# Expert results in one row per token and choice: a plain store that skips empty slots, in place of a scatter that adds into zeroed rows

## The chip, the core and the metric

The kernel runs on one core of a Trainium2 chip. The metric is device time in microseconds (us) of one launch; the time of a kernel is the median of several runs. One more run is recorded by the hardware profiler, and all rows below come from that one.

## The reference, cut to what matters

Two blocks of two layers each work on 512 tokens of width 1024. In the first block each layer has a mixer (fox attention, then mla, a latent attention) and a mixture of 16 experts, of which each token takes 2. The second block has a hyena mixer and a differential attention.

```
def hier_moe(h, w_grp, b_grp, w_rt, b_rt, w_gate, w_up, w_down):
    ...
    e_top, e_idx = lax.top_k(in_group, TOP_K_IN_GROUP)      # 2 of 16 experts for each of 512 tokens
    w = jax.nn.softmax(e_top, axis=-1) * g_top
    expert_id = g_idx * EXPERTS_PER_GROUP + e_idx
    combine = jnp.sum(jax.nn.one_hot(expert_id, N_EXPERTS, dtype=jnp.float32) * w[..., None], axis=1)
    a = jnp.einsum('td,edf->tef', t, w_gate)
    u = jnp.einsum('td,edf->tef', t, w_up)
    hidden = jax.nn.silu(a) * u * combine[..., None].astype(t.dtype)
    out = jnp.einsum('tef,efd->td', hidden, w_down)
...
    for i in range(DEPTH):
        ...                                                  # mixer: fox attention (i = 0), mla (i = 1)
        x = x + g1 * y
        h = rmsnorm(x, ffn_norm[i]) * (1.0 + sc2) + sh2
        x = x + g2 * hier_moe(h, ...)
# second block, on x and 16 meta tokens
    for i in range(DEPTH):
        y = rmsnorm_2(h, norm_pre[i])                        # then hyena (i = 0), differential attention (i = 1)
        ...
        h = h + rmsnorm_2(y, norm_post[i])
```

Only the mixture of experts, and the step that adds its result to x, are touched by the change. In all, 512 tokens with 2 choices make 1024 weighted expert results per layer, each a row of 1024 floats (4 KB).

## The kernel before

The work runs as one stream of stages on one core: fox attention (0 to about 345 us in the profile), the layer 0 mixture (routing to 410, 16 experts to 633), mla (to 905), the layer 1 mixture (routing to 965, experts to 1180, one overflow expert to 1207), hyena (to about 1890) and differential attention. TensorE multiplies in three passes with operands split in two halves (`whi` on ACT at L125, `wlo` on DVE at L128), so each 512 KB weight tile (`raw`, loaded at L133 by the SP queue) costs a cast on ACT and one on DVE.

**The mixture of experts.** `moe_head` writes the normed tokens to a DRAM table `hd`. Each expert has 128 slots, so 16 x 128 = 2048 slots hold 1024 results, and half of them are empty. The routing makes a table `tix` with the token of every slot; empty slots point to spare rows from 512 on. For each expert, POOL gathers the 128 rows (`xg`, L1206), PE transposes and multiplies (`expert_in`, `expert_out`), ACT copies the result to `yo` (one buffer, L1092), and POOL scatters the 128 rows to the DRAM table `yd` with an adding DMA (L1093). So that the adding has something to add to, `moe_fill` writes zeros to `yd` (640 rows of 4 KB) and to the spare rows of `hd` (128 rows), for each layer, during fox attention: its loop over head groups `g` calls it at g = 1 and g = 6, on the SP queue. Experts that overflow 128 slots are run behind the 16, in a block under a run-time condition (`tc.If`) and a loop. All engines pass the end of this block only when the DMAs before it have landed.

**The handover.** `moe_sum` (L1263) loads `yd` back in four tiles of 128 tokens (`y`, 512 KB each). `moe_norm` takes each: times the gate, added to x, square sum (DVE for the first tile, ACT for the others), a power on POOL, times the gain, and then eight transposes on PE (L374, `put_T`), which give the next stage's stationary operand. This step stands behind layer 0 (in `mla`) and behind layer 1 (in hyena). Hyena's filters (`hy_filter`, lines L1350 to L1412, tables `fsk` and `fk`, ending in the store `hs<-ht` by ACT's DMA queue) are computed along with the experts. The last of them is finished behind the block under the condition, at the start of the handover.

**What sets the order.** A list scheduler orders each engine's instructions at build time; each engine then runs its own in that order. DMAs of the SP queue are issued in that order too, and an instruction that must wait holds all that stand behind it on the same queue. DMAs take one of eight semaphores (DMAHW0 to 7) in turn, so a DMA can also wait for the one that used its semaphore before. Every phase (`Phase`) lays its tiles by tag into the same SBUF columns that the phase before used, and the build adds a wait where a new tile lies over an old one that is still read.

Of the kernel before, what the change touches and what calls it, by code (L numbers as in the profile page):

```python
# [20 lines left out]
S = 512  # L21
D = 1024
NT = S // 128
KD = D // 128
EPS = 1e-6
T = 528
# [4 lines left out]
FQ = 266  # L31
# [41 lines left out]
class Model:  # L73
# [264 lines left out]
    def moe_norm(self, ys, gain, hT, c0, tags, shift=None):  # L338


        nc, ph = self.nc, self.ph
        V = nc.vector

        def add(t):
            return V.tensor_add(self.x[t], self.x[t], ys[t])
        V.tensor_mul(ys[0], ys[0], self.g2)
        add(0)
        for t in range(NT):
            x, h = self.x[t], ys[t]
# [108 lines left out]
    def fox(self):  # L458
        nc, I, sm = self.nc, self.I, self.sm
        V, A = nc.vector, nc.scalar  # L460
        bufs = dict(raw=3, whi=4, wlo=4, un=24, qkv=8, P0=2, P1=2, P2=2, P3=1, PT=3, qT=3, kk=4, bias=2, sq=2, tmp=3, res=1, ada=2)
        with Phase(self, "fox", dict(mm=2, ad=1, pv=1, sc=2, tq=1, tp=1), bufs,
# [147 lines left out]
            for g in range(8):  # L610
# [93 lines left out]
    def mla(self):  # L704
        nc, I, sm = self.nc, self.I, self.sm
        V = nc.vector
        bufs = dict(raw=3, whi=4, wlo=4, h4=4, un=10, qk=16, v=2, qT=4, P0=2, P1=2, P2=2, P3=2, PT=3, sq=2, rot=2)
        with Phase(self, "mla", dict(mm=2, pv=1, sc=2, tq=2, tp=1), bufs,
# [7 lines left out]
            ys = [ph.t([128, D], F32, "qT", "y") for _ in range(NT)]  # L716
# [195 lines left out]
    def moe_consts(self):  # L912
# [9 lines left out]
        self.past = cp.tile([128, 1], F32, name="past")  # L922
        nc.vector.tensor_scalar(self.past, self.tok1[:, 0:1], float(S), None, op0=ALU.add)
# [11 lines left out]
        self.hd = [self.dr.tile([S + 128, D], F32, name=f"hd{l}") for l in range(2)]  # L935
        self.yd = [self.dr.tile([S + 128, D], F32, name=f"yd{l}") for l in range(2)]
        self.tabd = [self.dr.tile([128, 23, 2], F32, name=f"tabd{l}") for l in range(2)]

    def moe_fill(self, l):

        nc = self.nc
        zy = self.ph.t([128, 256], F32, "sq", "zy")
        nc.vector.memset(zy, 0.0)
        z = lambda n: zy[:, None, :].to_broadcast([128, n, 256])
        v = lambda a: a.rearrange("(p i) d -> p (i d)", p=128).rearrange("p (a b) -> p a b", b=256)
        nc.sync.dma_start(v(self.yd[l]), z(20))
        nc.sync.dma_start(v(self.hd[l][S:]), z(4))

    def moe_head(self, l, rows, work, bank):
# [22 lines left out]
        nc.sync.dma_start(self.hd[l][0:S].rearrange("(t p) d -> p t d", p=128), sh[:, None, :].to_broadcast([128, NT, D]))  # L972
# [103 lines left out]
    def expert_out(self, th, dn_w, idx, yd):  # L1076
# [14 lines left out]
        for c in range(2):  # L1091
            nc.scalar.copy(yo[:, c * 512:(c + 1) * 512], acc[c])  # L1092
        nc.gpsimd.indirect_dma_start(out=yd, out_offset=bass.IndirectOffsetOnAxis(ap=idx, axis=0),  # L1093
                                     in_=yo, in_offset=None, compute_op=ALU.add)

    def moe(self, l):
# [4 lines left out]
        with Phase(self, f"moe{l}", dict(dn=2, fl=2, mm=2, tp=2), bufs,  # L1101
# [61 lines left out]
            for i, (h, s_, w) in enumerate(((h1, s1, w1), (h2, s2, w2))):  # L1163
# [9 lines left out]
                V.tensor_mul(R[:, :, 0, :], R[:, :, 0, :], b(self.tok1, 23))  # L1173
# [6 lines left out]
            tf = ph.t([128, 23, 2], F32, "tf")  # L1180
            emp = ph.t([128, 23], F32, "emp")
            V.tensor_scalar(emp, ptv[:, 0, :], 0.0, self.past, op0=ALU.is_equal, op1=ALU.mult)
            V.scalar_tensor_tensor(tf[:, :, 0], emp, -1.0, ptv[:, 0, :], op0=ALU.add, op1=ALU.add)
            tix = ph.t([128, 23], I32, "tix")
            V.tensor_copy(tix, tf[:, :, 0])
# [35 lines left out]
            for e in range(16):  # L1221
# [13 lines left out]
                self.expert_out(th.pop(e), dw, tix[:, e:e + 1], yd)  # L1235
# [11 lines left out]
            with tc.If(n_any > 0):  # L1247
                tv = self.expert_in(self.slots_T(xg), lambda b: self.weights(wg[b]), tf[:, 16, 1:2])
                self.expert_out(tv, lambda b: self.weights(wd[b]), tix[:, 16:17], yd)
            with tc.For_i(1, n_ov, 1) as i:  # L1250
                e = nc.values_load(otab[0:1, ds(i, 1)], min_val=0, max_val=15)
                ri = ph.t([128, 2], F32, "ri")
                nc.sync.dma_start(ri, tabd[:, ds(i + 16, 1), :].rearrange("p o n -> p (o n)"))
                rx = ph.t([128, 1], I32, "rx")
                V.tensor_copy(rx, ri[:, 0:1])
                tv = self.expert_in(self.slots_T(gather(rx)), lambda b: self.weights(dyn(gu, b, e)), ri[:, 1:2])
                self.expert_out(tv, lambda b: self.weights(dyn(dn, b, e)), rx, yd)
# [172 lines left out]
    def hyena(self, done):  # L1430
# [5 lines left out]
        with Phase(self, "hy", dict(mm=2, tl=1, b1=3, tp=2), bufs,  # L1436
# [3 lines left out]
            home = ("ab", "H", "abT", "T4")  # L1440
            ys = [ph.t([128, 4, FQ], F32, h, "y").rearrange("p a b -> p (a b)")[:, :D] if h == "H" else
                  ph.t([128, D], F32, h, "y") for h in home]
# [715 lines left out]
```

## Time and profile before

| | us |
|---|---|
| median of 3 runs | 2627.5 (2625.51 to 2631.35) |
| the profiled execution's own time | 2622.27 |
| its span | 2620.5 |
| PE busy | 2384.9 (91%) |
| DVE busy | 1887.5 (72%) |
| ACT busy | 1507.4 (58%) |
| POOL busy | 255.4 (10%) |

PE is the busiest engine and is close to full in most stages; the DMA engines are busiest in the expert stages. A stage in which PE is full passes a delay at its start on to the end of the kernel.

### The profile page before, as it was taken

How to read it: one execution, taken by the hardware profiler on the slowest of the kernel's cores; microseconds unless marked ns; L12 is line 12 of the kernel's file. 1: busy time of each engine (PE TensorE's matmuls, PEld its weight loads, DVE VectorE, ACT ScalarE, POOL GpSimd, SP SyncE). 2: the span in 40 equal slices, each digit the busy share in tenths (PEclk: the TensorE clock that was granted, in tenths of full speed). 3: DMA queues.
4: the chain of work that ended last, by engine and by line, in shares of the span. 5: the costliest groups of instructions: out<-in, count | busy, mean ns of one | idle time of the engine just before them, and what ended most of it. 6: DMA issues, size and time to landing. Idle time of an engine off the chain costs nothing.

```text
span 2620.5 us, 40079 instructions
## 1 busy us (share of the span) xinstructions
PE 2384.9 (91%) x14775; PEld 1978.0 (75%) x14775; DVE 1887.5 (72%) x4037; ACT 1507.4 (58%) x2958; POOL 255.4 (10%) x264
## 2 busy tenths in 40 slices
PE   6889988897899979995999999999799999999988
PEld 5667767775766767774999999997577777777666
DVE  7888877886788768885566666664657778777755
ACT  5575757885567368874444444443336666665652
POOL 1100112221122022211000000000100000000000
PEclk8899989999899989997999999999899999999989
DMA  7776668997211289985323222224322121111232
GB/s 262 249 254 203 219 187 267 322 316 228 88 37 49 75 256 315 327 282 196 103 90 92 92 93 92 91 73 131 116 89 69 41 73 69 65 49 69 88 108 82
DMA packets 130271, 387.00 MB, mean 148 GB/s; under 512 B 23226, under 2 KB 34730, under 8 KB 129304
## 3 DMA queue, kind: packets, MB, share of 16 engines
q1 hardware_dynamic: 115640, 330.31, 37.1%
q0 software_dynamic: 12128, 45.38, 7.2%
q10 hardware_dynamic: 2304, 8.72, 0.8%
q8 instruction: 117, 1.92, 0.3%
q14 instruction: 82, 0.67, 0.1%
HBM read 330.58 MB, written 53.77 MB: 147 GB/s over the span
## 4 chain that ended last, share of the span: by engine, by line
PE 45%; DVE 4%; ACT 2%; issue 2%; DMA 1%; POOL 0%; POOLq 0%; SPq 0%; ACTq 0%; DVEq 0%
PE ps_mm L150 11%; PE ps_mm L151 10%; PE ps_mm L152 10%; PE ps_sc L1822 1%; PE ps_b L152 1%; PE ps_b L150 1%; PE ps_b L151 1%; PE ps_sc L1823 1%; PE ps_tp L1852 1%; ACT whi L125 1%; PE ps_tl L1764 1%; PE ps_tp L1565 1%; DVE wlo L128 1%; PE ps_pv L150 1%; PE ps_tq L1852 1%
## 5 line engine op out<-in xcount | busy, mean ns | idle before, releaser
L128 DVE TENSOR_TENSOR wlo<-raw,whi 128x1024 fp32r<-128x1024 f32 (+3 forms) x426 | 501.3, 1185 | 244.0 <-ACT whi L125 230.6
L125 ACT CAST whi<-raw 128x1024 fp32r<-128x1024 f32 (+3 forms) x426 | 433.2, 1022 | 246.9 <-PE ps_mm L152 91.1
L150 PE MATMUL ps_mm<-hT,whi 128*128 128x264 f32 x1024 | 294.7, 288 | 0.8 <-ACT hT L125 0.8
L151 PE MATMUL ps_mm<-hT,whi 128*128 128x264 f32 x1024 | 293.4, 287 | 0.8 <-DVE hT L128 0.8
L152 PE MATMUL ps_mm<-hT,wlo 128*128 128x264 f32 x1024 | 292.0, 285 | 0.0
L150 PE MATMUL ps_mm<-whi,hT 128*128 128x512 f32 x512 | 206.9, 406 | 6.9 <-DVE zg L1757 5.9
L151 PE MATMUL ps_mm<-wlo,hT 128*128 128x512 f32 x512 | 205.9, 403 | 0.0
L152 PE MATMUL ps_mm<-whi,hT 128*128 128x512 f32 x512 | 205.6, 403 | 0.0
L151 PEld LDWEIGHTS ps_mm<-hT,whi 128*128 128x128 f32 x1024 | 194.7, 190 | 1.1 <-DVE hT L128 1.1
L150 PEld LDWEIGHTS ps_mm<-hT,whi 128*128 128x128 f32 x1024 | 194.1, 190 | 1.6 <-ACT hT L125 1.6
L152 PEld LDWEIGHTS ps_mm<-hT,wlo 128*128 128x128 f32 x1024 | 194.4, 190 | 0.0
L151 PE MATMUL ps_mm<-wlo,un 128*128 128x384 f32 (+1 forms) x376 | 140.4, 375 | 10.0 <-DVE wlo L128 9.8
L150 PE MATMUL ps_mm<-whi,un 128*128 128x384 f32 (+1 forms) x376 | 141.4, 379 | 4.4 <-ACT whi L125 1.7
L152 PE MATMUL ps_mm<-whi,un 128*128 128x384 f32 (+1 forms) x376 | 138.3, 372 | 0.0
L1830 ACT ACTIVATE P<-P,nm 128x528 f32<-128x528 f32 x128 | 94.4, 737 | 70.7 <-DVE P L1827 69.1
L1499 ACT ACTIVATE u<-ps_mm,hb 128x264 f32<-128x264 f32 x96 | 46.2, 481 | 137.4 <-PE ps_mm L152 137.4
L119 POOL TENSOR_TENSOR r<-rs,mhalf 128x4 f32<-128x4 f32 (+1 forms) x72 | 79.1, 1102 | 400.1 <-DVE rs L118 381.5
L150 PEld LDWEIGHTS ps_mm<-whi,hT 128*128 128x128 f32 x512 | 97.0, 190 | 27.2 <-DVE zg L1757 6.8
L150 PE MATMUL ps_mm<-whi,xgT 128*128 128x512 f32 x264 | 107.1, 406 | 8.2 <-ACT xgT L125 8.2
L219 DVE CUSTOM_DVE_ANT_0 ada<-ada,crow 128x1024 f32<-128x1024 f32 x80 | 97.5, 1219 | 22.1 <-DMA ada<-in_w_ada_dram 21.4
L152 PEld LDWEIGHTS ps_mm<-whi,hT 128*128 128x128 f32 x512 | 97.0, 190 | 18.1
L151 PEld LDWEIGHTS ps_mm<-wlo,hT 128*128 128x128 f32 x512 | 96.8, 189 | 17.5 <-issue 0.2
(594 smaller groups left out, 6379.4 us busy)
## 6 DMA issues: line engine op xcount, KB each, us to landing
raw<-in_moe_gu_dram SPq DMA_DIRECT2D x136, 512.0 KB, 7.7
ada<-in_w_ada_dram SPq DMA_DIRECT2D x96, 512.0 KB, 4.3
raw<-in_moe_dn_dram SPq DMA_DIRECT2D x68, 512.0 KB, 7.0
raw<-in_hy_w_dram SPq DMA_DIRECT2D x64, 512.0 KB, 3.5
raw<-in_da_w_dram SPq DMA_DIRECT2D x64, 512.0 KB, 4.6
raw<-in_fox_w_dram SPq DMA_DIRECT2D x32, 384.0 KB, 4.6
hs<-ht ACTq DMA_DIRECT2D x16, 532.0 KB, 7.3
H<-hs SPq DMA_DIRECT2D x16, 532.0 KB, 3.4
```

Source lines behind the costliest of these rows:

```text
L119: self.lastpow = nc.gpsimd.tensor_tensor(out, t, self.mhalf[:in_.shape[0]].to_broadcast(list(in_.shape)), op=ALU.pow)
L125: nc.scalar.copy(hi, src)
L128: return nc.vector.tensor_sub(lo, src, hi.bitcast(F32))
L150: r = nc.tensor.matmul(o, a[0], b[0], start=first, stop=False)
L151: nc.tensor.matmul(o, a[0], b[1], start=False, stop=False)
L152: self.lastmm = nc.tensor.matmul(o, a[1], b[0], start=False, stop=last)
L219: nc.vector.tensor_tensor_reduce(out=t, in0=t, in1=self.crow, op0=ALU.mult, op1=ALU.add, scale=1.0, scalar=0.0, accum_out=v[:, j:j + 1])
L1499: A.activation(u[:, 1 + hs.start:1 + hs.stop], p, AF.Identity, bias=hb[:, c:c + 1])
L1565: nc.tensor.transpose(p[:, cs], ab[:, f, cs], self.ident)
L1764: nc.tensor.matmul(tp[32 * j:32 * j + 16, 0:64], xt[:, k, :], w[:, c0 + j * 64:c0 + (j + 1) * 64], start=(k == 0), stop=(k == KD - 1))
L1830: nc.scalar.activation(P, P, AF.Exp, bias=nm_, scale=-1.0, accum_out=sum_)
L1852: nc.tensor.transpose(p[0:n, qt * 128:(qt + 1) * 128], Ps[qt][:, kt * 128:kt * 128 + n], self.ident)
```

## The change

`yd` gets 1024 rows, one per token and choice: the second choice of token t has row 512 + t. Each expert's 128 rows are stored without adding; a slot that is empty has an index past the end of the table, and the bounds check of the indirect DMA leaves its row out. Gathers leave empty slots out in the same way, and the first three `xg` buffers of a layer are set to 0 on DVE, so that slots never written hold no garbage. No table is filled with zeros any more. `moe_sum` loads two tiles per token tile, and `moe_norm` adds them on DVE. The second tile of each pair needs a place: in mla a buffer of tag `PT`; in hyena the tags `fsk`, `s` (two halves), `g` (two halves) and the back half of `T4`.

```
@@ moe_norm
+        def both(t):
+            y, pieces = ys[t]
+            n = D // len(pieces)
+            for i, p in enumerate(pieces):
+                V.tensor_add(y[:, i * n:(i + 1) * n], y[:, i * n:(i + 1) * n], p)
+            V.tensor_mul(y, y, self.g2)
...
-        V.tensor_mul(ys[0], ys[0], self.g2)
+        both(0)
         add(0)
...
-                V.tensor_mul(ys[t + 1], ys[t + 1], self.g2)
+                both(t + 1)
@@ fox attention
-                if g == 1:
-                    self.moe_fill(0)
-                if g == 6:
-                    self.moe_fill(1)
@@ mla
-            ys = [ph.t([128, D], F32, "qT", "y") for _ in range(NT)]
+            ys = [(ph.t([128, D], F32, "qT", "y"), [ph.t([128, D], F32, "PT", "y2")]) for _ in range(NT)]
@@ tables
-        self.hd = [self.dr.tile([S + 128, D], F32, name=f"hd{l}") for l in range(2)]
-        self.yd = [self.dr.tile([S + 128, D], F32, name=f"yd{l}") for l in range(2)]
+        self.hd = [self.dr.tile([S, D], F32, name=f"hd{l}") for l in range(2)]
+        self.yd = [self.dr.tile([2 * S, D], F32, name=f"yd{l}") for l in range(2)]
...
-    def moe_fill(self, l):
...
-        nc.sync.dma_start(v(self.yd[l]), z(20))
-        nc.sync.dma_start(v(self.hd[l][S:]), z(4))
@@ expert_out
         nc.gpsimd.indirect_dma_start(out=yd, out_offset=bass.IndirectOffsetOnAxis(ap=idx, axis=0),
-                                     in_=yo, in_offset=None, compute_op=ALU.add)
+                                     in_=yo, in_offset=None, bounds_check=2 * S - 1, oob_is_err=False)
@@ moe
-                V.tensor_mul(R[:, :, 0, :], R[:, :, 0, :], b(self.tok1, 23))
+                V.tensor_mul(R[:, :, 0, :], R[:, :, 0, :], b((self.tok1, self.tok2)[i], 23))
...
+            V.tensor_scalar(emp, tf[:, :, 0], S - 0.5, -float(S), op0=ALU.is_gt, op1=ALU.mult)
+            V.tensor_add(tf[:, :, 2], tf[:, :, 0], emp)
...
+                if len(self.gathered) < 3:
+                    V.memset(xg, 0.0)
                 r = nc.gpsimd.indirect_dma_start(out=xg, out_offset=None, in_=hd,
-                                                 in_offset=bass.IndirectOffsetOnAxis(ap=idx, axis=0))
+                                                 in_offset=bass.IndirectOffsetOnAxis(ap=idx, axis=0),
+                                                 bounds_check=S - 1, oob_is_err=False)
@@ moe_sum
-        self.nc.sync.dma_start(y, self.yd[l][t * 128:(t + 1) * 128, :])
+        whole, pieces = y
+        r = self.yd[l][t * 128:(t + 1) * 128, :]
+        self.nc.sync.dma_start(whole, r)
+        r, n = self.yd[l][S + t * 128:S + (t + 1) * 128, :], D // len(pieces)
+        for i, p in enumerate(pieces):
+            self.nc.sync.dma_start(p, r[:, i * n:(i + 1) * n])
@@ hyena
-            home = ("ab", "H", "abT", "T4")
...
+            t4 = ph.t([128, 4, 2, FQ], F32, "T4", "y").rearrange("p a b c -> p (a b c)")
+            two = lambda tag: [ph.t([128, T], F32, tag, "y2")[:, :512] for _ in range(2)]
+            ys = [(ph.t([128, D], F32, "ab", "y"), [ph.t([128, D], F32, "fsk", "y2")]),
+                  (ph.t([128, 4, FQ], F32, "H", "y").rearrange("p a b -> p (a b)")[:, :D], two("s")),
+                  (ph.t([128, D], F32, "abT", "y"), two("g")), (t4[:, :D], [t4[:, D:2 * D]])]
```

The first place is the SP queue (it issues DMAs alone) at the handover after layer 1. The names: `y<-yd_105` is the load of a token tile of layer 1, `gain` the next norm's gain, `raw` hyena's weights; 128x1024 is 512 KB. Before:

```order
L1263 DMA y<-yd_105 128x1024
L278 DMA gain<-in_norm_pre_dram 128x1024
L1263 DMA y<-yd_105 128x1024 x3
L133 DMA raw<-in_hy_w_dram 128x1024 x2
L133 DMA raw<-in_hy_w_dram 128x1024 [waits DMAHW1_49]
```

In the changed kernel, `y_13431` and so on are the second tiles (the row without a number is the fourth tile's pair, which shares one buffer):

```order
L1267 DMA y<-yd_105 128x1024
L1270 DMA y_13431<-yd_105 128x1024 [waits DVE_49,PE_49]
L278 DMA gain<-in_norm_pre_dram 128x1024
L1267 DMA y<-yd_105 128x1024
L1270 DMA y_13433<-yd_105 128x512
L1270 DMA y_13434<-yd_105 128x512
L1267 DMA y<-yd_105 128x1024
L1270 DMA y_13436<-yd_105 128x512 [waits DMAHW1_49]
L1270 DMA y_13437<-yd_105 128x512 [waits DMAHW2_49]
L1267 DMA y<-yd_105 128x1024 [waits DMAHW3_49]
L1270 DMA y<-yd_105 128x1024 [waits DMAHW4_49]
L133 DMA raw<-in_hy_w_dram 128x1024 [waits DMAHW5_49]
```

Four loads became ten, all ahead of the first weights; the second of them waits for DVE and PE, and the eighth row of the list for DMAHW1, which belongs to the store `hs<-ht`.

The second place is DVE at the same handover, first token tile, with the semaphores that each instruction waits for. Before:

```order
L346 TENSOR_TENSOR y<-y,gate 128x1024 [waits DMAHW2_49]
L345 TENSOR_TENSOR x_136<-x_136,y 128x1024 [waits DVE_49]
L354 ISA y,ss<-x_136 128x1024 [waits DVE_49]
L354 ISA ss 128x1
L359 TENSOR_TENSOR y<-y,gate 128x1024 [waits DMAHW4_49]
```

After:

```order
L348 TENSOR_TENSOR y<-y,y_13431 128x1024 [waits DMAHW3_49,DMAHW2_49]
L349 TENSOR_TENSOR y<-y,gate 128x1024 [waits DVE_49]
L352 TENSOR_TENSOR x_136<-x_136,y 128x1024 [waits DVE_49]
L361 ISA y,ss<-x_136 128x1024 [waits DVE_49]
L361 ISA ss 128x1
L348 TENSOR_TENSOR y<-y,y_13433 128x512 [waits DMAHW6_49,DMAHW5_49]
```

An addition that waits for two loads, the second of them on DMAHW3, now stands ahead of the gate's product.

The third place is the SP queue at the handover after layer 0 (`A`, `sh`: scale and shift of the next norm; `raw`: mla's weights). Before:

```order
L1263 DMA y<-yd_104 128x1024
L278 DMA A<-modd_2199 128x1024
L278 DMA sh<-modd_2199 128x1024
L1263 DMA y<-yd_104 128x1024
L133 DMA raw<-in_mla_w_dram 128x2x336
L1263 DMA y<-yd_104 128x1024
L133 DMA raw<-in_mla_w_dram 128x2x336
L1263 DMA y<-yd_104 128x1024 [waits DMAHW7_49]
L133 DMA raw<-in_mla_w_dram 128x2x336 [waits DMAHW0_49]
```

After:

```order
L1267 DMA y<-yd_104 128x1024
L1270 DMA y_7102<-yd_104 128x1024
L278 DMA A<-modd_2195 128x1024
L278 DMA sh<-modd_2195 128x1024
L1267 DMA y<-yd_104 128x1024
L1270 DMA y_7104<-yd_104 128x1024
L133 DMA raw<-in_mla_w_dram 128x2x336
L1267 DMA y<-yd_104 128x1024 [waits DMAHW3_49]
L1270 DMA y_7106<-yd_104 128x1024 [waits DMAHW4_49]
L133 DMA raw<-in_mla_w_dram 128x2x336 [waits DMAHW5_49]
L1267 DMA y<-yd_104 128x1024 [waits DMAHW6_49]
L1270 DMA y_7108<-yd_104 128x1024 [waits DMAHW7_49,DVE_49]
```

Before, the fourth tile's load waited for a semaphore (DMAHW7, of the store `hs<-ht`); now the third tile's does (DMAHW3), and more loads stand behind it.

## Rows read from the trace of the kernel before

**Rows 1.** Windows: stretch, length, busy time of PE, PEld, DVE, ACT, POOL; clock, DMA share, GB/s.

```profile
120.00:345.00 225.00, 205.66 (x1136) 161.17 (x1135) 191.06 (x474) 151.65 (x335) 28.93 (x24) 0.98 0.70 227
410.00:633.00 223.00, 204.05 (x1033) 165.55 (x1032) 180.41 (x275) 176.16 (x292) 47.48 (x38) 0.99 0.93 299
965.00:1180.00 215.00, 200.68 (x1022) 161.92 (x1021) 176.45 (x266) 174.21 (x288) 50.50 (x39) 1.00 0.95 309
1246.00:1700.00 454.00, 451.94 (x3644) 443.87 (x3643) 279.32 (x456) 202.38 (x389) 0.00 (x0) 1.00 0.28 92
```

**Rows 2.** Timeline of the handover after layer 0.

```profile
633.37 1.56 POOL L1093 DMA_INDIRECT yd<-yo,tix  x1 [5.59 <-ACT yo L1092]
...
637.01 0.57 ACT L1409 ACTIVATE ht<-ps_fl,fnd,finv 128x266 f32<-128x266 f32 x1 [0.93 <-PE ps_fl L1407]
...
640.78 0.35 SPq L1263 DMA_DIRECT2D y<-yd  x1
...
644.74 1.23 DVE L346 TENSOR_TENSOR y<-y,gate 128x1024 f32<-128x1024 f32 x1 [3.43 <-DMA y<-yd]
...
653.00 1.11 PE L374 MATMUL ps_tq<-ident,y 128*128 128x128 f32 x4 [7.02 <-DVE y L362]
...
653.69 0.32 SPq L1263 DMA_DIRECT2D y<-yd  x1
```

**Rows 3.** The same timeline, further on: fourth token tile.

```profile
677.75 0.66 PE L374 MATMUL ps_tq<-ident,y 128*128 128x128 f32 x4 [0.67 <-DVE y L362]
```

**Rows 4.** The chain that ended last, 1160 to 1250: start, length, what.

```profile
1200.52 6.15 DMA yd<-yo,tix
```

**Rows 5.** Timeline of the handover after layer 1.

```profile
1207.47 0.34 SPq L1263 DMA_DIRECT2D y<-yd  x1
...
1208.34 1.40 SPq L1263 DMA_DIRECT2D y<-yd  x3
...
1209.78 15.14 SPq L133 DMA_DIRECT2D raw<-in_hy_w_dram  x3
...
1214.33 1.23 DVE L346 TENSOR_TENSOR y<-y,gate 128x1024 f32<-128x1024 f32 x1
...
1220.88 0.48 PE L1407 MATMUL ps_fl<-fsk,fk 73*128 73x266 f32 x1
...
1221.91 0.33 ACTq L1412 DMA_DIRECT2D hs<-ht  x1
...
1222.22 1.09 PE L374 MATMUL ps_tp<-ident,y 128*128 128x128 f32 x8 [0.86 <-DVE y L360]
...
1245.58 0.63 PE L374 MATMUL ps_tp<-ident,y 128*128 128x128 f32 x4 [4.41 <-DVE y L360]
```

**Rows 6.** DMA issues: queue, count, KB each, median us from issue to landing.

```profile
hs<-ht ACTq DMA_DIRECT2D x16, 532.0 KB, 7.3
...
hd<-htok POOLq DMA_DIRECT2D x8, 512.0 KB, 7.2
...
x1d<-h POOLq DMA_DIRECT2D x4, 512.0 KB, 3.0
...
yd<-yo,tix POOLq DMA_INDIRECT x33, 9.7
```

**Rows 7.** Line L1263 (first loads of the expert results).

```profile
DMA to landing us min/median/max: 3.2/6.1/10.1
```

**Rows 8.** Waits in fox attention, 120 to 345: us, times, longest.

```profile
DVE ada L219 <- DMA ada<-in_w_ada_dram: 17.5, 19, 2.2
...
PE ps_mm L151 <- DVE wlo L128: 6.1, 5, 2.4
...
PE ps_tq L571 <- DVE qT L128: 2.9, 1, 2.9
```

**Rows 9.** Waits among layer 1's experts, 965 to 1180.

```profile
ACT yo L1092 <- DMA yd<-yo,tix: 6.3, 4, 2.9
```

**Rows 10.** Waits from 382 to 690, the routing and experts of layer 0.

```profile
DVE xgT L1058 <- ACT full L1056: 3.9, 2, 3.7
```

More of the change, by code (lines that the diff above doesn't have):

```diff
@@ L920, in moe_consts @@
                        allow_small_or_imprecise_dtypes=True)
-        self.past = cp.tile([128, 1], F32, name="past")
-        nc.vector.tensor_scalar(self.past, self.tok1[:, 0:1], float(S), None, op0=ALU.add)
+        self.tok2 = cp.tile([128, NT], F32, name="tok2")
+        nc.vector.tensor_scalar(self.tok2, self.tok1, float(S), None, op0=ALU.add)
         self.desc16 = cp.tile([128, 16], F32, name="desc16")
@@ L933, in moe_consts @@
         nc.gpsimd.memset(self.onesb, 1.0)
-        self.hd = [self.dr.tile([S + 128, D], F32, name=f"hd{l}") for l in range(2)]
-        self.yd = [self.dr.tile([S + 128, D], F32, name=f"yd{l}") for l in range(2)]
-        self.tabd = [self.dr.tile([128, 23, 2], F32, name=f"tabd{l}") for l in range(2)]
-    def moe_fill(self, l):
[L941 to L945, printed above, removed]
-        nc.sync.dma_start(v(self.yd[l]), z(20))
-        nc.sync.dma_start(v(self.hd[l][S:]), z(4))
+        self.hd = [self.dr.tile([S, D], F32, name=f"hd{l}") for l in range(2)]
+        self.yd = [self.dr.tile([2 * S, D], F32, name=f"yd{l}") for l in range(2)]
+        self.tabd = [self.dr.tile([128, 23, 3], F32, name=f"tabd{l}") for l in range(2)]
     def moe_head(self, l, rows, work, bank):
@@ L1179, in moe @@
             ptv = pt.rearrange("p (a b) -> p a b", a=2)
-            tf = ph.t([128, 23, 2], F32, "tf")
+            tf = ph.t([128, 23, 3], F32, "tf")
             emp = ph.t([128, 23], F32, "emp")
-            V.tensor_scalar(emp, ptv[:, 0, :], 0.0, self.past, op0=ALU.is_equal, op1=ALU.mult)
+            V.tensor_scalar(emp, ptv[:, 0, :], 0.0, 4096.0, op0=ALU.is_equal, op1=ALU.mult)
             V.scalar_tensor_tensor(tf[:, :, 0], emp, -1.0, ptv[:, 0, :], op0=ALU.add, op1=ALU.add)
-            tix = ph.t([128, 23], I32, "tix")
-            V.tensor_copy(tix, tf[:, :, 0])
+            V.tensor_scalar(emp, tf[:, :, 0], S - 0.5, -float(S), op0=ALU.is_gt, op1=ALU.mult)
+            V.tensor_add(tf[:, :, 2], tf[:, :, 0], emp)
+            tix, tox = ph.t([128, 23], I32, "tix"), ph.t([128, 23], I32, "tox")
+            V.tensor_copy(tix, tf[:, :, 2])
+            V.tensor_copy(tox, tf[:, :, 0])
             self.routed = V.tensor_copy(tf[:, :, 1], ptv[:, 1, :])
@@ L1234, in moe @@
                 dw = lambda b: self.weights(dn[e, b])
-                self.expert_out(th.pop(e), dw, tix[:, e:e + 1], yd)
+                self.expert_out(th.pop(e), dw, tox[:, e:e + 1], yd)
                 while have < (2 * e + 2) * along // 32:
@@ L1248, in moe @@
                 tv = self.expert_in(self.slots_T(xg), lambda b: self.weights(wg[b]), tf[:, 16, 1:2])
-                self.expert_out(tv, lambda b: self.weights(wd[b]), tix[:, 16:17], yd)
+                self.expert_out(tv, lambda b: self.weights(wd[b]), tox[:, 16:17], yd)
             with tc.For_i(1, n_ov, 1) as i:
                 e = nc.values_load(otab[0:1, ds(i, 1)], min_val=0, max_val=15)
-                ri = ph.t([128, 2], F32, "ri")
+                ri = ph.t([128, 3], F32, "ri")
                 nc.sync.dma_start(ri, tabd[:, ds(i + 16, 1), :].rearrange("p o n -> p (o n)"))
-                rx = ph.t([128, 1], I32, "rx")
-                V.tensor_copy(rx, ri[:, 0:1])
+                rx, ro = ph.t([128, 1], I32, "rx"), ph.t([128, 1], I32, "ro")
+                V.tensor_copy(rx, ri[:, 2:3])
+                V.tensor_copy(ro, ri[:, 0:1])
                 tv = self.expert_in(self.slots_T(gather(rx)), lambda b: self.weights(dyn(gu, b, e)), ri[:, 1:2])
-                self.expert_out(tv, lambda b: self.weights(dyn(dn, b, e)), rx, yd)
+                self.expert_out(tv, lambda b: self.weights(dyn(dn, b, e)), ro, yd)
             for _ in fil:
```

8 lines of the change are left out of this document (3 added, 5 removed).

## The prediction

> **What bounds the kernel now.** I read the windows by stage first, to see where PE is full [rows 1]. In 1246 to 1700, hyena, PE is busy for 451.94 of 454 us, so whatever delays hyena's start delays the end by the same amount. Among the experts PE is busy for 204.05 of 223 us and 200.68 of 215 us, while the DMA engines stand at 0.93 and 0.95 of their time. That looks like a DMA bound, but the idle PE there comes to only 19.0 + 14.3 us in all. In fox attention, where the zero fills are written, PE has 205.66 of 225 us and the DMA share is 0.70. Second I read the timelines of the two handovers, where PE waits for DVE, and DVE for loads [rows 2, 3, 5]. Third, the chain of waits (the last store of layer 1 is on it, [rows 4]), and last the landing times and the waits by line [rows 6 to 10]. So the change has four places where it can count: the fills in fox attention, the traffic among the experts, and the two handovers.
>
> **Fox attention: no fills.** Per layer 640 + 128 rows of 4 KB go, 3.1 MB, 6.3 MB in all. At the 299 and 309 GB/s that the experts' stages reach [rows 1] that is about 21 us of the DMA engines' time. It counts only where PE waits for it. DVE waits 17.5 us for `ada` loads there, 2.2 at most at a time, but PE waits only 6.1 us for `wlo` and 2.9 for `qT`, which DVE makes late [rows 8]. These 9.0 us bound the gain; the scheduler also issues the loads of this stage in a different order, which can cost as much as one such wait of 2.9. I take **-3**, between -8 and +3.
>
> **Routing and experts.** Three small DVE operations in the routing, and three memsets of 128x1024 a layer, which cannot cost more than the 1.23 us of a product of that shape [rows 2]: 3.7 us if nothing covered them. DVE waits 3.9 us for ACT at the first transposed slots [rows 10], and that covers them; without that cover it is +3.7 a layer. A gather and a store move half of their 128 rows, so some 33 x 2 x 0.26 = 17 MB less, 57 us of DMA time at 305 GB/s. PE does not wait for transfers there by its rows; what a faster store takes from the path is the wait of ACT's `yo` copy for the store before it, 6.3 us in layer 1 [rows 9], the longest of them (2.9) at the last expert, where the matmuls ahead of it end just before the copy starts. I take **-1** for both layers, between -4 and +4.
>
> **When the handovers start.** The last store is issued at 633.37 and the first load at 640.78 [rows 2]; behind layer 1 the landing takes 6.15 us from 1200.52 to 1206.67, and the load follows 0.8 later, at 1207.47 [rows 4, 5]. No row has an indirect store without adding. Its nearest rows: a plain 512 KB store from POOL lands in 3.0 us, an adding one in 7.2 and the scatter in 9.7, all medians [rows 6]. Bounds are 6.15 (no gain) and 3.0. I take the lower end, since the adding is the difference between the two rows of equal size; then layer 1's handover starts 3.1 us earlier at best, and I take 2.5, for the 128 separate rows. In layer 0 something else then ends last: ACT ends at 637.01 + 0.57 = 637.58, and the load comes at about 638.4, 2.4 earlier.
>
> The Trainium skill ("DMA: Bandwidth & Descriptors", Anatomy of one DMA) gives a POOL-issued transfer about 2.0 us plus its bytes at 436 GB/s, whether it adds or not: 3.2 us for 512 KB. The plain store's 3.0 agrees, the scatter's 6.15 does not. If the time went by bytes alone, halving them would gain 0.6 us a handover, and the sum below would be 3.7 us higher.
>
> **Handover after layer 0.** The first tile now needs two loads and an addition. One more 0.52 MB at 305 GB/s is 1.7, the addition 1.23: the first transposes come 2.9 us later relative to the first load (653.00 - 640.78 = 12.2 before). Further on, the second load, of the fourth tile in the kernel before, waited until 653.69, because its semaphore was the one of the `hs` store [rows 2]. Now the third tile's load has such a semaphore, and two weight loads and three more tiles stand behind it on SP: 4 x 0.52 + 2 x 0.34 = 2.8 MB, which is 9 us of transfer after a release at about 13 us from the start, so 22 us from the start. The weights there were issued one and two microseconds after 653.69 before and land some 4 us later now. The fourth tile's transposes at 677.75 (37.0 after the start, [rows 3]) should come 5 us later by this; with none of it on the path 2.4 are gained, with all of it 4.6 lost. Net 5.0 - 2.4 = **+2.6**, between -2 and +5.
>
> **Handover after layer 1.** This is the large term. SP issued the four tile loads within 2.3 us of 1207.47 [rows 5], and they landed while PE was busy with the last filter. Now the second DMA in the list waits for PE. Its place is tag `fsk`, which lies over columns that the last filter's tables used; their last reader is the fourth L1407 matmul, 1220.88 + 0.48 = 1221.36, which is 13.9 us after the start. Behind the waiting DMA stand the gain, the other eight tile loads, three weight tiles, and the biases: everything that hyena starts with. Step by step, from the start of the handover: the second tile is issued at 13.9 and lands at 17.1 with the shortest landing of such a load, 3.2 [rows 7]. From the gate's product (1214.33) to the first transposes (1222.22) DVE and POOL took 7.9; with the addition 9.1. First transposes at 26.2, against 14.75 before: 11.5 later. The rest of the queue, 11 x 0.52 = 5.8 MB, needs 19 us at 305 GB/s, until 33 from the start; the seventh tile load also waits for the `hs` store, 1221.91 + 7.3 [rows 6] = 21.7 from the start, while 2.6 MB ahead of it are on their way until about 22.5, so that wait is covered. From the first to the fourth transposes it was 23.4 us (1222.22 to 1245.58), part of it waiting for weights and a store. If that distance stays, the fourth transposes come 11.5 us later; if the waits in it go but three additions come, it is about 9; if the weights that land at 33 hold ACT, which casts them ahead of the third tile's square, up to 15. Behind the fourth transposes PE is full. Net 11.5 - 2.5 = **+9**, between +3 and +15.
>
> The Trainium skill (same page, Bandwidth) has 425 GB/s for one core's large loads. By it the 5.8 MB would be there at about 27.5 rather than 33, and the upper end of this term would fall to about +9; no window here shows more than 309.
>
> **The sum.** -3 - 1 + 2.6 + 9 = +7.6 against the profiled execution: 2622.3 + 7.6 = 2629.9. The median of the runs is 2627.5, 5.2 above that execution, so I predict **2635**.
>
> **The rivals.**
>
> *The transfers were the bound after all (faster).* The mechanism: with DMA at 0.93 to 0.95, weights come a little late everywhere, ACT and DVE cast them late, and PE's 33.3 idle us are the end of that. If 24 MB less took half of that idle time (17 us) and 6 us in fox attention, the sum would be -17 - 6 + 11.6 = -11: about 2616. It decides from about 17 us of gain in these stages on (+11.6 for the handovers, 5.3 for the bound of measurement). For it speaks the DMA share; against it the waits, where PE waits for ACT and DVE and hardly for a transfer. If a third is taken, it is 2622. Chance 0.17.
>
> *It cancels (same).* The late loads of layer 1 are half hidden: the hold lasts as said, but the distance of the tiles shrinks to DVE's work, and stores land 3 us earlier. Then the handovers give about +4 together and the rest -4: 2627.5. Chance 0.27.
>
> *The store gains nothing (slower still).* The 128 separate rows and the bounds check set the landing, not the adding; then the 4.9 us from both handover starts are missing, and the sum is +12.5: 2640. For it speaks that the scatter's POOL time is 1.6 us in [rows 2] whatever its rows do; against it the pair of plain and adding stores. Chance 0.14.
>
> The forecast has the remaining 0.42; its own range is 2631 to 2641.
>
> **How the numbers follow.** This kernel's runs differ by some 0.2%, about 5.3 us, and less cannot be told from no change. Faster by more has the first rival's 0.17. Within it lie the second rival and a small share of the forecast's lower end, 0.28 with the rounding. Slower has the rest, 0.55. The range takes the first rival's weaker form at its lower end and the third's case with a late layer 1 at its upper: 2620 to 2646.
>
> **What would show it.** In the changed kernel SP should issue one tile load at the start of the handover after layer 1, then nothing for about 14 us; DVE's addition should wait for that load; the transposes of the first tile should stand about 26 us after the first load, the fourth's about 49. Last stores should land in about 3 us. The expert windows should keep their lengths within 2 us while their DMA share falls. The forecast is wrong if the expert windows shrink by several us each, if the second load does not hold the queue, or if fox attention changes by more than 8 us.

## The result and the profile after

The changed kernel takes **2641.93 us** (median of 8 runs, 2638.38 to 2644.48), the kernel before 2622.93 over 8 runs (2616.63 to 2631.35), the three on record before among them. The ratio is **1.0074**, interval 1.0060 to 1.0089: slower, by some 19 us. The profiled execution has a span of 2642.8 us against 2620.5.

Windows of the profile after, stage by stage; columns as in [rows 1]:

```profile
410.00:633.00 223.00, 200.49 (x975) 162.19 (x976) 178.36 (x271) 170.35 (x278) 40.09 (x37) 0.97 0.77 258
973.00:1188.00 215.00, 197.38 (x974) 158.83 (x973) 175.73 (x264) 169.45 (x277) 40.50 (x39) 0.97 0.78 265
1214.04:1265.40 51.36, 20.43 (x80) 16.34 (x80) 33.16 (x48) 17.70 (x32) 10.85 (x21) 0.60 0.71 258
1265.40:1720.00 454.60, 452.89 (x3641) 445.10 (x3642) 278.60 (x454) 202.11 (x389) 0.00 (x0) 0.99 0.29 93
```

Among the experts the DMA share fell from 0.93 and 0.95 to 0.77 and 0.78, as the change intends, and PE is busy for a little less of the same length than in [rows 1]. The start of hyena became a stretch of 51 us with PE busy for 20. From there on hyena runs as before.

The table cuts both spans at the same places: the last `hd` store of a layer (L984, now L977), the expert stores on POOL, the first load on SP, the fourth tile's transposes. It is worked out from the starts in the two timelines.

| stretch, us | before | after | predicted | measured |
|---|---|---|---|---|
| fox attention, to the last `hd` store | 381.3 | 375.7 | -3 | -5.6 |
| layer 0: routing and experts, to the last store | 252.0 | 260.6 | -1, both layers | +8.6 |
| (of it to the second store) | 61.0 | 70.7 | | +9.7 |
| last store to first load | 7.4 | 5.6 | -2.4 | -1.8 |
| first load to fourth tile | 37.0 | 43.5 | +5.0 | +6.5 |
| mla | 253.1 | 251.7 | 0 | -1.4 |
| layer 1: routing and experts | 269.6 | 273.4 | (above) | +3.7 |
| (of it to the second store) | 64.9 | 73.2 | | +8.3 |
| last store to first load | 6.9 | 3.5 | -2.5 | -3.4 |
| first load to fourth tile | 38.1 | 51.4 | +11.5 | +13.3 |
| hyena and the rest | 1374.9 | 1377.4 | 0 | +2.5 |
| sum | 2620.5 | 2642.8 | +7.6 | +22.3 |

Handover after layer 1, timeline after (against [rows 5]):

```profile
1214.04 0.34 SPq L1267 DMA_DIRECT2D y<-yd  x1
...
1227.52 0.48 PE L1414 MATMUL ps_fl<-fsk,fk 73*128 73x266 f32 x1
...
1228.03 0.33 SPq L1270 DMA_DIRECT2D y<-yd  x1
...
1232.34 1.22 DVE L348 TENSOR_TENSOR y<-y,y 128x1024 f32<-128x1024 f32 x1 [11.47 <-DMA y<-yd]
...
1235.39 0.79 SPq L1270 DMA_DIRECT2D y<-yd  x2
...
1240.41 1.97 PE L381 MATMUL ps_tp<-ident,y 128*128 128x128 f32 x8 [12.42 <-DVE y L367]
...
1265.43 1.94 PE L381 MATMUL ps_tp<-ident,y 128*128 128x128 f32 x8 [4.94 <-DVE y L367]
```

One load goes out, then SP stands still for 14.0 us until the last reader of `fsk` is through (1227.52 + 0.48 = 1228.00). DVE's first addition waits for that load. The first tile comes 26.4 us after the first load, the fourth 51.4 us; about 26 and 49 were forecast. A second gap on SP, before 1235.39, is the wait for the `hs` store that the prediction named and thought covered by transfers. Here it is: in windows of 1 and 2 us from 1231 to 1246 the DMA engines stand at 0.93 to 1.04 of their time, across the gap. It comes back below.

Handover after layer 0 (against [rows 2, 3]):

```profile
636.35 0.97 POOL L1086 DMA_INDIRECT yd<-yo,tox  x1 [5.70 <-ACT yo L1085]
...
641.99 0.34 SPq L1267 DMA_DIRECT2D y<-yd  x1
...
655.34 0.33 SPq L1267 DMA_DIRECT2D y<-yd  x1
...
685.47 0.66 PE L381 MATMUL ps_tq<-ident,y 128*128 128x128 f32 x4 [0.55 <-DVE y L369]
```

The third tile's load waits for the `hs` store until 13.35 us after the first load, as said, and the fourth tile comes 6.5 us later relative to it.

What the prediction did not have is the +9.7 and +8.3 before the second store of a layer. Timeline after, in the routing of layer 0:

```profile
375.73 0.90 POOL L977 DMA_DIRECT2D hd<-htok  x1 [0.30 <-POOL htok L976]
...
399.34 0.16 DVE L1181 CAST tix<-tf 128x23 int32<-128x23 f32 x1
...
402.99 0.91 DVE L1205 MEMSET xg<- 128x1024 f32 x1 [0.15 <-issue]
...
404.19 3.63 POOL L1206 DMA_INDIRECT xg<-hd,tix  x1 [26.98 <-DVE th L1066]
407.81 0.62 POOL L1342 DMA_DIRECT2D fst<-fstd  x1
...
409.37 0.44 PE L1074 MATMUL ps_tp<-ident,th 128*128 128x128 f32 x2
415.53 1.25 PE L1377 MATMUL ps_fl<-fst,fw 128*128 128x264 f32 x4 [5.72 <-DMA fst<-fstd]
416.58 0.63 PE L152 MATMUL ps_mm<-whi,xgT 128*128 128x512 f32 x1
417.00 0.63 PE L150 MATMUL ps_mm<-whi,xgT 128*128 128x512 f32 x1
...
427.31 1.17 POOL L1086 DMA_INDIRECT yd<-yo,tox  x1 [5.60 <-ACT yo L1085]
...
446.45 1.02 POOL L1086 DMA_INDIRECT yd<-yo,tox  x1 [16.04 <-ACT yo L1085]
```

The same in the kernel before, from the last `hd` store to the second expert store:

```profile
381.32 0.90 POOL L984 DMA_DIRECT2D hd<-htok  x1 [0.30 <-POOL htok L983]
...
417.82 0.75 PE L1370 MATMUL ps_fl<-fst,fw 128*128 128x264 f32 x4 [2.06 <-DMA fst<-fstd]
418.41 0.40 PE L152 MATMUL ps_mm<-whi,xgT 128*128 128x512 f32 x1
418.64 0.39 PE L150 MATMUL ps_mm<-whi,xgT 128*128 128x512 f32 x1
...
442.33 1.82 POOL L1093 DMA_INDIRECT yd<-yo,tix  x1 [11.66 <-ACT yo L1092]
```

The list of slots (`tix`) is ready at 399.5. The gather could go then, but its buffer is cleared by a memset that DVE reaches only at 402.99, behind two weight casts. The gather starts when the memset is done (its row names the DVE instruction right behind it), and behind the gather on POOL's queue stands the load of the filter table `fst`, which is not the experts' at all. PE reaches the filter matmul at 409.8 and waits 5.72 us for that table; the kernel before has this wait too, of 2.06 us. After the idle time the matmuls start 0.43 us apart and take 0.63 each, where the kernel before has 0.23 and 0.39: PE runs at the lower of its two clock levels, 1.2 instead of 2.4 GHz. From 420.0 on they are 0.23 apart again, but the clock falls twice more ahead of the second store, from 430.4 to 433.8 and from 441.7 to 443.9. Windows of the same stretch, first gather to second store, after and then before:

```profile
404.20:446.50 42.30, 32.77 (x154) 26.87 (x153) 28.36 (x42) 25.70 (x46) 11.14 (x10) 0.84 0.72 217
```

```profile
405.10:442.30 37.20, 32.40 (x187) 27.21 (x186) 29.63 (x49) 29.71 (x54) 11.00 (x9) 1.00 0.90 270
```

A granted clock of 0.84 against 1.00. Counted from the last `hd` store, the change is 3.3 us behind when the filter matmul starts, 5.5 at the first store (427.31, before 427.35 after an `hd` store 5.6 later) and 9.7 at the second: the wait itself is the smaller part. Of the rest, 21 steps from one 128x512 matmul to the next at 0.43 us instead of 0.23 make 4.2. In layer 1 it is the same again: PE waits for `fst` by 6.6 us, where before it did not wait for it at all.

### The profile page after: what moved, and what is told of

It is laid out like the page before. It is cut to its first block, busy times and chain, and to the rows that moved or that the text cites. A ratio compares the mean times of both kernels' runs of the same rounds, so it can differ in the third digit from the quotient of the medians.

```text
span 2642.8 us, 40166 instructions
## 1 busy us (share of the span) xinstructions
PE 2393.4 (91%) x14775; PEld 1985.8 (75%) x14775; DVE 1902.6 (72%) x4057; ACT 1507.8 (57%) x2958; POOL 240.7 (9%) x264
## 5 line engine op out<-in xcount | busy, mean ns | idle before, releaser
L150 PE MATMUL ps_mm<-whi,xgT 128*128 128x512 f32 x264 | 109.9, 416 | 8.7 <-ACT xgT L125 8.7
L152 PE MATMUL ps_mm<-whi,xgT 128*128 128x512 f32 x264 | 108.9, 412 | 3.1 <-DVE xgT L128 3.0
```

Source lines behind the costliest of these rows:

```text
L150: r = nc.tensor.matmul(o, a[0], b[0], start=first, stop=False)
L152: self.lastmm = nc.tensor.matmul(o, a[1], b[0], start=False, stop=last)
```

## Experiments

Each was timed over 5 rounds beside the kernel before. Ratios are to that kernel; 0.001 is 2.6 us. Differences between two kernels are told as differences of their ratios; where the intervals overlap, that is said.

| kernel | median us | ratio (95%) |
|---|---|---|
| the change | 2641.93 | 1.0074 (1.0060 to 1.0089) |
| e1_no_hold | 2636.84 | 1.0059 (1.0045 to 1.0073) |
| e6_pool_memset | 2626.30 | 1.0023 (1.0013 to 1.0032) |
| e2_full_gather | 2621.85 | 1.0009 (1.0000 to 1.0018) |
| e9_early_memset | 2624.76 | 1.0003 (0.9995 to 1.0012) |
| e3_fills | 2645.97 | 1.0098 (1.0081 to 1.0115) |
| e4_plain | 2610.66 | 0.9961 (0.9948 to 0.9974) |
| e8_add_bounded | 2613.23 | 0.9966 (0.9953 to 0.9980) |
| e5_both | 2616.36 | 0.9984 (0.9976 to 0.9993) |
| e7_sp_order | 2611.43 | 0.9968 (0.9956 to 0.9980) |
| e10_early_sp | 2615.85 | 0.9976 (0.9965 to 0.9987) |

**The held queue alone.** The second load of layer 1's first tile goes to a place nobody reads.

```
-            ys = [(ph.t([128, D], F32, "ab", "y"), [ph.t([128, D], F32, "fsk", "y2")]),
+            ys = [(ph.t([128, D], F32, "ab", "y"), [ph.t([128, D], F32, "wlo", "y2")]),
```

> The changed kernel, with the second tile of the first token tile in layer 1's handover placed in a buffer of tag wlo instead of fsk, so that its load waits for nothing; the order of every engine's instructions is the same as in the changed kernel. Theory (the held SP queue costs the handover): SP issues the second load right behind the first, the first transposes come about 16 us after the first load instead of 26, and the kernel gets 6 to 11 us faster than the changed one (2642), to about 2631 to 2636; the eighth DMA still waits for the store of the filters, so not all of the 13 us come back. Rival (the bytes of the second tiles and the four additions cost it, not the hold): the first transposes stay beyond 22 us and the time stays within 3 us of 2642.

Measured: 0.0015 less than the change, 4 us where 6 to 11 were expected; the intervals overlap, so the times alone don't show the gain. Timeline of this kernel's handover:

```profile
1210.07 0.34 SPq L1267 DMA_DIRECT2D y<-yd  x1
1210.45 0.43 SPq L1270 DMA_DIRECT2D y<-yd  x1
...
1225.00 1.09 PE L381 MATMUL ps_tp<-ident,y 128*128 128x128 f32 x8 [1.08 <-DVE y L367]
...
1227.16 0.80 SPq L1270 DMA_DIRECT2D y<-yd  x2
...
1238.97 1.94 PE L381 MATMUL ps_tp<-ident,y 128*128 128x128 f32 x8 [12.88 <-DVE y L367]
...
1258.54 1.94 PE L381 MATMUL ps_tp<-ident,y 128*128 128x128 f32 x8 [5.19 <-DVE y L367]
```

The first tile is back at 14.9 us after the first load, so the hold did what was said of it. But the eighth DMA, the third tile's second load, takes the semaphore of the `hs` store, and SP stands still again until 17.1 us after the start, with the weights behind. The fourth tile comes at 48.5 instead of 51.4. In the change transfers cover this wait; here the loads that went out early have landed by 1220 (the DMA share is 0.01 from there to 1224.5), and the wait stands bare. One hold stood in front of another, and taking the first away uncovers the second.

**The memset: its engine, its presence, its place.** First the same memset on POOL:

```
-                    V.memset(xg, 0.0)
+                    nc.gpsimd.memset(xg, 0.0)
```

> The changed kernel, with the three settings to 0 of the xg buffers on POOL, which is idle there, instead of DVE. Theory (DVE does the memset behind two weight casts, so the first gather and the filter tables' load behind it on POOL start late, PE waits, and its clock falls): the first gather is issued within 1 us of its indices in both layers, PE's wait for the table fst falls from 5.7 and 6.6 us to 2 and 0, and the kernel is 5 to 9 us faster than the changed one, about 2633 to 2637. Rival (the gathers that leave empty slots out are themselves late or the order of the filter work is at fault): the first gather is as late as before this edit, or the time stays within 3 us of 2642.

Measured: 13 us less than the change, more than was expected: the wait for `fst` went from 5.7 to 1.7 us, and in layer 1 from 6.6 to 0.7. Then no memset: all 128 rows are gathered, and an empty slot takes the token of its own number.

```
+            own = ph.t([128, 23], F32, "own")
+            V.tensor_scalar(own, ptv[:, 0, :], 0.0, self.tok1[:, 0:1], op0=ALU.is_equal, op1=ALU.mult)
...
-                if len(self.gathered) < 3:
-                    V.memset(xg, 0.0)
...
-                                                 bounds_check=S - 1, oob_is_err=False)
```

> The changed kernel with gathers that read all 128 rows (an empty slot reads the row of its own number), with no bounds check and no memset; stores still leave empty slots out. Theory of the memset: like the kernel with the memset on POOL, 5 to 9 us faster than the changed one, and a little less if the 8 MB that the gathers move again cost something; 2633 to 2638. Rival (relief of the DMA engines by the smaller gathers is worth several us): no faster than 2640, although the first gather is early.

Measured: 17 us less than the change, where 5 to 9 were expected, and no wait for `fst` in layer 0. Windows of this kernel, first gather to second store of each layer:

```profile
404.50:437.10 32.60, 30.18 (x176) 25.39 (x176) 27.91 (x44) 28.35 (x53) 9.14 (x9) 1.00 0.97 300
...
954.80:988.60 33.80, 30.63 (x177) 25.61 (x176) 28.45 (x47) 28.91 (x54) 7.69 (x9) 1.00 0.86 288
```

The clock is 1.00 again and the stretch 9.7 us shorter, though all the gathers' bytes are back. Last, the small gathers with one memset a layer, early on POOL:

```
+            slot = [ph.t([128, D], F32, "xg", n) for n in ("full", "full", "xg")]
+            nc.gpsimd.memset(slot[2], 0.0)
             picked = {0: self.slots_pick(head[:, 0, :], slot[0])}
...
-                xg = ph.t([128, D], F32, "xg")
-                if len(self.gathered) < 3:
-                    V.memset(xg, 0.0)
+                xg = ph.t([128, D], F32, "xg") if self.gathered else slot[2]
```

> The changed kernel with one memset a layer instead of three (the other two buffers were filled whole by the picked slots before), and that one on POOL, ahead of the routing's end, in a buffer that is set aside for the first gather; the gathers leave empty slots out as in the changed kernel. If the place of the memset (late on DVE, with POOL's queue behind it) is what cost the 17 us: 2622 to 2625, the second store of layer 0 some 59 us after the last hd store, and no wait of PE for fst. If the gathers with empty slots left out cost something by themselves: 2630 or more.

Measured: 0.0071 less than the change, 19 us. Its timeline at the place where the change waited:

```profile
373.92 1.26 POOL L1132 MEMSET xg<- 128x1024 f32 x1
...
400.35 2.90 POOL L1204 DMA_INDIRECT xg<-hd,tix  x1 [24.64 <-DVE ot L1191]
403.25 0.62 POOL L1340 DMA_DIRECT2D fst<-fstd  x1
...
409.35 0.44 PE L1073 MATMUL ps_tp<-ident,th 128*128 128x128 f32 x2
410.06 0.76 PE L1375 MATMUL ps_fl<-fst,fw 128*128 128x264 f32 x4 [0.28 <-DMA fst<-fstd]
410.66 0.39 PE L152 MATMUL ps_mm<-whi,xgT 128*128 128x512 f32 x1
...
419.59 1.29 POOL L1085 DMA_INDIRECT yd<-yo,tox  x1 [6.67 <-ACT yo L1084]
```

The list of slots is ready and PE is at the same point at the same time as in the change (399.5 in both; 409.35 and 409.37), `fst` is asked for 4.6 us earlier, the wait is 0.28, and the first store is issued at 419.59 instead of 427.31. So it is the place of the memset, with POOL's queue behind it. It is not DVE's time, and empty slots in a gather cost nothing either. The held load of hyena's start is still in this kernel and in e2_full_gather: the fourth tile's transposes come 50.3 and 50.9 us after the first load, 51.4 in the change. Even so their times are those of the kernel before (1.0003 and 1.0009), which matters for the account below.

**The fills put back**, into tables that nobody reads:

```
+                if g == 1:
+                    self.moe_fill(0)
+                if g == 6:
+                    self.moe_fill(1)
```

> The changed kernel, with the zero fills of before written during fox attention, to tables that nobody reads. Theory (the fills slowed fox attention): the last store of the normed tokens in layer 0, at 375.7 us in the changed kernel and 381.3 before, moves back to about 381, and the time grows by 3 to 6 us, to about 2645 to 2648. Rival (the fills are hidden, and the 5.6 us came from the scheduler's other order or from elsewhere): the stage keeps its end at about 376 and the time its 2642.

Measured: 0.0024 more than the change, 6 us (4 by the medians; the intervals overlap a little). The trace has it in fox attention: the last `hd` store at 379.9 instead of 375.7. A single trace says less than that: over four traces with fills it lies between 379.9 and 385.9, over eight without between 373.3 and 378.4.

**The store: adding, or the number of rows.** Two edits of the kernel before. One drops the adding and keeps the 128 rows, so that the two choices of a token are not summed; the other keeps the adding and drops the empty rows.

```
-                                     in_=yo, in_offset=None, compute_op=ALU.add)
+                                     in_=yo, in_offset=None)
```

> The kernel before with the adding taken out of its stores (all 128 rows are still stored, to the same 640 row table; the sum over a token's two choices is left out, the later store wins). If the adding sets the landing (the prediction's reading): the stores land in 3 to 4 us instead of 6.1, layer 1's handover starts about 3.5 us after the last store instead of 6.95, layer 0's about 5.6 instead of 7.4, and the whole is 2616 to 2619 against 2623. If the separate rows set it: landings stay near 6, and the time stays within 2 us of before.

```
-                                     in_=yo, in_offset=None, compute_op=ALU.add)
+                                     in_=yo, in_offset=None, compute_op=ALU.add,
+                                     bounds_check=S - 1, oob_is_err=False)
```

> The kernel before with a bound on its adding stores, so that the empty slots' rows are left out: half the rows, still adding. If the adding sets the landing: 5 us or more, and a time of 2621 to 2624. If the number of rows sets it: about 3 to 3.5 us, and a gain of 4 to 6 us as with plain stores. The DMA share of the experts' stages falls in either case, and their lengths stay within 2 us.

Measured: both gain 9 to 10 us by the ratios. The last store of layer 1 in the chain that ended last, in the plain kernel, the bounded one, and a later experiment, e7_sp_order, which has neither the adding nor the empty rows ([rows 4] has the 6.15 of before):

```profile
1194.60 4.25 DMA yd<-yo,tix
```

```profile
1200.51 4.31 DMA yd<-yo,tix
```

```profile
1186.52 2.51 DMA yd<-yo,tox
```

For this store it was neither one alone: the adding costs 1.8 to 1.9 us and the empty rows 1.7 to 1.8, together 3.6. But it is the overflow expert's, and nearly all of its slots are empty: with the bound it writes 0.03 of 0.52 MB. The store of the 16th expert just ahead of it, which keeps 0.27 MB, in the kernel before, the plain and the bounded one:

```profile
1180.40 6.09 DMA yd<-yo,tix
```

```profile
1176.24 3.37 DMA yd<-yo,tix
```

```profile
1179.08 5.88 DMA yd<-yo,tix
```

In e7_sp_order it is 3.22. The last store of layer 0, which keeps 0.16 MB, lands in 6.5, 3.5 and 5.9 us, and in 3.1 in the change. So for an expert of the usual kind the adding costs 2.7 to 3.0 us and the empty rows 0.2 to 0.6. The handover starts follow: from the last store to the first load it takes, in layer 0, 7.41 us before, 5.57 plain, 6.87 bounded, 5.64 in the change; in layer 1, 6.95, 5.06, 5.11, 3.51.

These starts make 3.7 us of the plain kernel's gain and 2.4 of the bounded one's. Where the rest of the 9 to 10 us lies is not shown: the two traces are of executions 7 us above their kernel's median, and their spans are only 4.8 and 2.6 us below the one before. From its second to its last store of layer 0 the bounded kernel takes 188.8 us, against 191.0 before and 189.9 in the change.

**The repairs together.** The full gathers and the free place of the second load, the two diffs above in one kernel:

> The changed kernel with the full gathers without memsets, and the second load of layer 1 in a place that nobody holds. The two gains belong to different stages and should add: 2621.9 less some 4 to 5, so 2616 to 2618. If they don't add (the freed start of layer 1 is taken up by the wait for the hs store's semaphore as before): 2621 to 2623.

Measured: 2616.36, within the range in which they add. The fourth tile of hyena comes 43.7 us after the first load. In e1_no_hold it was 48.5 with the same list on SP; there the loads landed later (DVE waited 3.71 us for the small `cw` load, here not at all), and why is not settled.

For the next step, on top of this, hyena's loads were written in another order, the second tile's second load as one DMA in another free place (`wlo`):

```
-            raws = {z: self.raw(I["hy_w"][0, z]) for z in (1, 2, 0)}
...
+                for z in ((), (1, 2), (0,), ())[t]:
+                    raws[z] = self.raw(I["hy_w"][0, z])
```

> As the last one, and SP's list in hyena's start is rearranged: the second tile's second load is one whole DMA in a free place, and two weight tiles come before the third tile, so that the eighth DMA, which waits for the hs store, is the third tile's load. If that wait is what still stretches the start of hyena: the fourth transposes come at about 40 to 44 us after the first load instead of 48.5, and the time is 2609 to 2614. If the three more additions on DVE set the distance: the fourth stays at 47 to 49, and the time within 2 us of the last one's.

Measured: 2611.43, faster than the change and than the kernel before. Its handover after layer 1:

```profile
1189.83 0.34 SPq L1266 DMA_DIRECT2D y<-yd  x1
...
1192.13 0.98 SPq L133 DMA_DIRECT2D raw<-in_hy_w_dram  x2
...
1207.50 0.33 SPq L1266 DMA_DIRECT2D y<-yd  x1
...
1232.16 1.94 PE L381 MATMUL ps_tp<-ident,y 128*128 128x128 f32 x8 [5.11 <-DVE y L367]
```

SP still waits for the `hs` store, until 17.7 us, but now two weight tiles are ahead of the wait. The fourth tile is at 42.3, within the 40 to 44 expected, yet only 1.3 better than in e5_both, though the medians differ by 4.9. So the order of the list has the smaller part of the expected effect in this stretch. Against the 38.1 of before 4.2 are left; DVE's additions, 3.7 us for three tiles of 1.23, are the likely rest, which no run separates.

And this list with the early memset and the small gathers, in place of the full ones:

> The same with hyena's loads in the order of the SP list experiment. If the smaller gathers are worth nothing and the two repairs add: 2610 to 2613, as with the full gathers. If half the gathers' bytes help the experts' stages: below 2608.

Measured: 2615.85, above the 2610 to 2613 expected; the ratio is 0.9976 against 0.9968 with full gathers, intervals overlapping. In its trace PE waits for `fst` again, by 1.0 and 1.6 us. No gain from leaving empty slots out of the gathers is seen here.

## Why the prediction was right, and where it was not

**The direction was right, but not for the reason given.** Slower was forecast because hyena's start waits behind a held queue. That wait is there as described: the hold lasted 14.0 us (13.9 forecast), the first tile came at 26.4 (26.2), the fourth at 51.4 (49.6), +13.3 where +11.5 stood. But it does not decide the sign. e9_early_memset and e2_full_gather keep the hold and lose what the memsets cost, and they take as long as the kernel before (by their intervals, at most 5 us longer). Without that cost the other terms cancel, as the second rival had it; in the change's own trace they leave 4.3 of the 22.3 us. What makes the change slower by 19 us is the memsets, which the forecast put at nothing. That the time lies in the range, whose upper end came from the third rival with a late layer 1, is luck for the same reason.

**The hold and the wait behind it.** Taking the hold away by itself gave back only 4 us in the timed runs; with the memsets gone it gave 6.6 (e5_both against e2_full_gather), with SP's list changed as well 10.7. The prediction had seen the second wait, on the `hs` store, and called it covered by transfers. In the change it is; without the hold it is not. The rate that it took for them, 305 GB/s, was too low: it says that no window shows more than 309, but the windows of [rows 1] are means over 200 us and more. In windows of 2 us from 1232 to 1244 the change moves 396 to 418 GB/s, and the kernel before 420 to 422 from 1214 to 1218.

**The step that failed** is in "Routing and experts": "DVE waits 3.9 us for ACT at the first transposed slots [rows 10], and that covers them". The memsets were costed as DVE time, 3.7 us a layer at worst, and laid beside a DVE wait. But they are not paid in DVE's time. A gather waits for the first one, POOL's queue waits behind the gather, PE for the table behind that, and then PE's clock falls. That is +9.7 and +8.3 us to the second store, and +12.3 for the two layers as a whole, where -1 stood, outside its range of -4 to +4. For the held load the prediction named everything that is queued behind it; for the memset it did not. "PE does not wait for transfers there by its rows" was not so either: in the trace before, PE waits 2.06 us for that very table in layer 0, so a later gather falls straight on PE. Layer 1 gave 4.6 back between its second and its last store. The plain stores do the same there (198.5 us against 204.7; 204.0 with bounded adding stores), so it goes with the adding. It is not only the waits of [rows 9], 6.3 us: they are gone in the change, but in the bounded kernel they fall too, to 1.7, and the stretch keeps its length. What the adding holds up there is open.

**Handover starts**: -1.8 and -3.4 against -2.4 and -2.5. The choice of 3.0 us for the landing was near (3.1 for the last store of layer 0 in the change; 2.7 is the least of all its stores). The reason given, the adding, holds behind layer 0; behind layer 1, where the overflow expert's store comes last, the empty rows count as much. By the formula of the Trainium skill ("DMA: Bandwidth & Descriptors", Anatomy of one DMA), which has no term for adding, an estimate for 512 KB is 3.2 us. The plain stores of 512 KB shown above, 3.4 to 4.25 us, are near it; the adding ones, 6.1 to 6.5, do not agree.

**Fox attention**: -5.6 in one trace; putting the fills back costs 4.2 in its trace and 4 to 6 us in time: the right sign, more than the size, inside the range. Which wait it came from is open, and it is not the two of PE that [rows 8] names: in the change `wlo` goes from 6.1 to 5.4 us and `qT` from 2.9 to 5.7.

**Handover after layer 0**: +6.5 against +5.0, by the steps named.

**The rivals.** That transfers were the bound is refuted three times: in the change itself, with full gathers, and with bounded adding stores. From the second to the last store of layer 0 it is 191.0 us before (DMA share 0.92), 189.9 in the change (0.77), 188.2 with the full gathers and 188.8 with bounded stores (0.85): the lengths do not follow the traffic. That the store gains nothing is refuted by both handover starts.

**The number.** The sum was +7.6; the traces differ by 22.3 and the medians by 19.0. That 2635 lies only 7 us from the result is partly luck: the median it started from, 2627.5, was 4.6 above that of all 8 runs of the kernel before. From 2622.93 the sum leads to 2630.5, 11.4 short, which is nearly the +13.3 by which the routing and experts missed.

## What to carry to other kernels

A cheap instruction is priced by what waits for it, not by its own engine's spare time: follow the wait to the next queue, and list what stands behind it there, also work that has nothing to do with the change. Where two waits stand one behind the other in a DMA queue, removing the first shows the second; count both before promising a gain. And a change that bundles several edits is best taken apart: here one bound on the adding store is worth 9 us by itself (0.9966), and the full change with three details put in other places is no better by more than the noise (e7_sp_order, 2611 us, 0.9968).

## What had not been expected of the hardware

- After an idle time of 5.72 us PE's matmuls of 128x512 came 0.43 us apart for eight steps and then 0.23 again. In the same stretch (granted clock 0.84) they fell back to 0.43 twice more, behind waits of 0.98 and 0.81 us and behind one of 2.00. In the kernel before, waits of 2.06, 0.86 and 1.54 us at these places left them at 0.23. So the length of one wait doesn't tell here whether the clock falls, and a first wait 3.7 us longer went with a stretch to the second store 9.7 us longer.
- POOL's own time for an indirect store goes with the adding, not with the rows: medians of 1614 ns before and 1615 bounded, 995 plain and 1018 in the change. The landing goes mostly with the adding (2.7 to 3.0 us of 6.1 to 6.5 at the end of each layer's 16 experts), and with the rows where nearly all are empty.
